# The intra-chunk levels of the gated recurrent heads: products of 64 columns per chunk against products of 128 columns per pair of chunks

## The chip, the cores and the metric

The kernel runs on one core of a Trainium2 chip. The metric is the device time of one execution in microseconds. Three runs of the kernel before took 2513.89, 2510.45 and 2513.90 us; their median is 2513.89 us. A profile of one further execution is read beside them.

The core has four compute engines that run their own queues in order and wait for one another on semaphores: TensorE (PE, matrix products, with a separate weight load, PEld, for each), VectorE (DVE), ScalarE (ACT) and GpSimd (POOL). DMA transfers are issued mostly from SyncE (SP).

## The reference

One transformer-like block over 512 tokens and 2048 features. What bears on this case is the HGRN2 head group: 8 heads of width 128, a gated linear recurrence over the tokens.

```python
qf = silu(q);  log_f = log(lb + (1 - lb) * sigmoid(f_pre));  kf = (1 - lb) * sigmoid(-f_pre)
b = cumsum(log_f within a chunk)
# inside a chunk, for t >= s, per channel k of the head:
att[t, s] = sum_k q[t, k] * kf[s, k] * exp(b[t, k] - b[s, k])
out[t] = sum_s att[t, s] * v[s] + (q[t] * exp(b[t])) @ state
state  = exp(b_last) * state + sum_s (kf[s] * exp(b_last - b[s])) v[s]^T
```

Around it stand a modulated norm, an input projection of 7184 columns, a Mamba-2 head group (SSD), a gate and output projection, and a gated feed-forward network with 5632 hidden features. Everything is float32.

## The kernel before

**Projections.** Every large product is computed in float32 accuracy out of three products of a faster type. `wchunk` (L139) loads two 128-row pieces of a weight into a `raw` buffer, casts them to a high part on ACT (`whi`, L161) and forms the low part on DVE (`wlo`, L162); two buffers each hold them. `mm3` (L165 to L168) then issues three matmuls of 512 columns into a PSUM accumulator: high by high, high by low, low by high. `feat_group` (L621) and `tok_group` (L643) run over the weight's chunks; a chunk is eight calls of `mm3`.

**Small work between the large.** After each `mm3` the kernel calls `small()` (L601). Two generators are active at a time, taken from a list `waiting`; `small()` lets one of them issue its next step, in turn, and a generator that has yielded n sits out n calls. So the products of the recurrent heads (`hgrn_mix`, L526) and of the SSD heads (`ssd_mix`) are strewn singly between projection products. Per chunk, `tick()` (L214) advances the modulation sums (`mod_unit`, L174): each step fetches 512 KB of `w_mod` into a `raw` buffer and adds it up on DVE in `macc` (L187, L189). `rate` sets how many steps a chunk makes: 0.5 while the heads' f and q columns are projected, 1.5 from the z groups on. The order in which the groups run is: the first projection segments, the second v group, four groups for f and q of two heads each, two z groups, two gate groups, the output projection, the feed-forward network. The engines' queues are ordered when the kernel is built: among the instructions that the builder's model holds ready, the one that stands earliest in the program goes first.

**A recurrent head.** `hgrn_f` and `hgrn_q` (L514 to L524) turn the projected columns, which lie as 128 channels by 512 tokens, into the gate `f`, the key `k` and the query `q`. In `hgrn_mix` the tokens form four chunks of 128. The pair products of a chunk are built in levels 1, 2, 4, ..., 64. At level lv, tokens are taken in blocks of 2 lv: the queries of a block's second half meet the keys of its first half. So per level and chunk there is one product (L547) with `k` of the chunk, 128 columns, as weights, and the 64 second-half queries of the chunk as the moving operand. The four results fill 256 columns of one PSUM bank. Then DVE does four things: it multiplies the second-half queries by the gate product of the first half (L552), the first-half keys by that of the second half (L553), copies from PSUM into `att` under a mask that keeps each block's own pairs (L555), and multiplies the two gate products of a block into one (L557), in place, so that the running products stand at every 2 lv-th token (`tcur`). After the seven levels `k` holds what the state needs and `q` what meets the state. Then come the transposes of `k` (L563), the state products with `v` (L570), the state sums on DVE (L573, L575), and the output products, `att` by `v` and `q` by state (L581, L584), copied out by ACT (L589).

**Buffers.** `T()` (L65) takes tiles from a ring of nine of 512 columns, shared by `q`, `att`, `Kt`, `st` and the z and gate groups' `zs`, `gs`. `MIS()` (L77) takes one of two PSUM banks for all small products. `f` and `k` of two heads share an `FK` tile, two of which exist together with the SSD heads' `xdt`. The projections have six PSUM banks.

**Masks.** `level_masks` (L666) builds one int8 mask of 128 x 256 per level on POOL (L672, L674).

Of the kernel before, what the change touches and what calls it, by code (L numbers as in the profile page):

```python
# [34 lines left out]
def hybrid_block_kernel(  # L35
# [55 lines left out]

    ident = CT([P, P], "ident")
    make_identity(nc, ident)
    ones = CT([P, P], "ones")
    V.memset(ones, 1.0)
    tri = CT([P, P], "tri")
# [414 lines left out]
    def ov(t):  # L511
        return otile[t // 2].rearrange("p (t f) -> p t f", t=2)[:, t % 2, :]

    def hgrn_f(ps, h, f, k):  # L514
        A.activation(out=f, in_=ps, func=AF.Sigmoid)
        V.tensor_scalar(out=f, in0=f, scalar1=omlT[:, h:h + 1], scalar2=lbT[:, h:h + 1], op0=ALU.mult, op1=ALU.add)
        A.activation(out=k, in_=ps, func=AF.Sigmoid, scale=-1.0)
        V.tensor_scalar(out=k, in0=k, scalar1=omlT[:, h:h + 1], scalar2=None, op0=ALU.mult)

    def hgrn_q(ps):  # L520
        q = T("q")
        A.activation(out=q, in_=ps, func=AF.Sigmoid)
        V.tensor_tensor(out=q, in0=q, in1=ps, op=ALU.mult)
        return q  # L524

    def hgrn_mix(h, f, k, q):  # L526
# [9 lines left out]
                        in1=ident.unsqueeze(1).broadcast_to([P, 4, P]), op=ALU.mult)  # L536
        V.tensor_tensor(out=q, in0=q, in1=f, op=ALU.mult)
        yield 2
        tcur = f
        for lv in LEVELS:  # L540
            nb = S // (2 * lv)
            ps = MIS()
            npc = P // (2 * lv)
            qv = q.rearrange("p (b two j) -> p b two j", two=2, j=lv)
            kv = k.rearrange("p (b two j) -> p b two j", two=2, j=lv)
            for cch in range(4):
                PE.matmul(out=ps[:, cch * 64:(cch + 1) * 64], lhsT=k[:, cch * P:(cch + 1) * P],  # L547
                          rhs=qv[:, cch * npc:(cch + 1) * npc, 1, :], start=True, stop=True)
                if cch < 3:
                    yield 0  # L550
            tv = tcur.rearrange("p (b two) -> p b two", two=2)
            V.tensor_tensor(out=qv[:, :, 1, :], in0=qv[:, :, 1, :], in1=bc(tv[:, :, 0], [P, nb, lv]), op=ALU.mult)  # L552
            V.tensor_tensor(out=kv[:, :, 0, :], in0=kv[:, :, 0, :], in1=bc(tv[:, :, 1], [P, nb, lv]), op=ALU.mult)  # L553
            av = att.rearrange("p (b two j) -> p b two j", two=2, j=lv)[:, :, 1, :]
            V.copy_predicated(out=av, mask=lmask[lv].rearrange("p (b j) -> p b j", j=lv),  # L555
                              data=ps[:, 0:256].rearrange("p (b j) -> p b j", j=lv))
            V.tensor_tensor(out=tv[:, :, 0], in0=tv[:, :, 0], in1=tv[:, :, 1], op=ALU.mult)  # L557
            tcur = tv[:, :, 0]
            yield 2
        kt_ = T("Kt")[:, 0:3 * P]  # L560
        ps = MIS()
        for cch in range(3):
            PE.transpose(out=ps[:, cch * P:(cch + 1) * P], in_=k[:, cch * P:(cch + 1) * P], identity=ident)  # L563
            yield 0
        A.copy(out=kt_, in_=ps[:, 0:3 * P])
        yield 1
# [6 lines left out]
        V.tensor_copy(out=st[:, 0:P], in_=ps[:, 0:P])  # L573
        for cch in (1, 2):
            V.scalar_tensor_tensor(out=st[:, cch * P:(cch + 1) * P], in0=st[:, (cch - 1) * P:cch * P],  # L575
                                   scalar=tcur[:, cch:cch + 1], in1=ps[:, cch * P:(cch + 1) * P],
                                   op0=ALU.mult, op1=ALU.add)
        po = MIS()
        for cch in range(4):
            sl = slice(cch * P, (cch + 1) * P)  # L580
            PE.matmul(out=po[:, sl], lhsT=att[:, sl], rhs=vt[:, cch, :], start=True, stop=(cch == 0))  # L581
            yield 0
            if cch > 0:
                PE.matmul(out=po[:, sl], lhsT=q[:, sl], rhs=st[:, (cch - 1) * P:cch * P], start=False, stop=True)  # L584
                yield 0
        if not otile:
            otile.extend([E(name="o"), E(name="o")])
# [6 lines left out]
            A.activation(out=junk, in_=ov(cch)[:, h * P:(h + 1) * P], func=AF.Square, accum_out=sq[:, cch:cch + 1])  # L594
        r = rstd_of(sq, 4, P)
        V.tensor_copy(out=orstd[:, h, :], in_=r)


    active, waiting = [], []
# [61 lines left out]
    def bl(i):  # L661
        return slice(i * P, (i + 1) * P)
# [3 lines left out]
    def level_masks():  # L666
        one8 = tmp.tile([P, 256], I8, tag="t", name="one8")
        V.memset(one8, 1)
        for h in LEVELS:
            nb = P // (2 * h)  # L670
            m = CT([P, 256], f"lm{h}", I8)
            G.affine_select(out=m, in_=one8, pattern=[[0, 4], [-2 * h, nb], [0, h]], base=0,  # L672
                            channel_multiplier=1, compare_op=ALU.is_ge, fill=0.0)
            G.affine_select(out=m, in_=m, pattern=[[0, 4], [2 * h, nb], [0, h]], base=h - 1,  # L674
                            channel_multiplier=-1, compare_op=ALU.is_ge, fill=0.0)
            lmask[h] = m


# [94 lines left out]
    for pr in range(4):  # L773
        h0 = 2 * pr
        rate[0] = 0.5
        accs = feat_group([(C_F + P * h0, 256), (C_Q + P * h0, 256)], [bl(i) for i in range(4)])
        fkt = E(name="FK", tag="a").rearrange("p (a s) -> p a s", a=4)
        for i in range(2):
            f_, k_ = fkt[:, 2 * i, :], fkt[:, 2 * i + 1, :]
            hgrn_f(accs[i], h0 + i, f_, k_)  # L780
            waiting.append(hgrn_mix(h0 + i, f_, k_, hgrn_q(accs[2 + i])))
# [256 lines left out]
```

## Time and profile before

| quantity | value |
| --- | --- |
| median of three runs | 2513.89 us |
| profiled execution, its own time | 2516.08 us |
| profiled execution, span | 2514.4 us |
| mean granted clock of TensorE | 0.988 |
| first and last level product (L547) | 469.4 and 794.7 us |
| last copy of a head's output (L589) | 824.4 us |
| level products: instructions, mean duration | 448, 251 ns |

The profile counts an instruction as busy from its start to its (modelled) end; consecutive matmuls overlap, so that starts, not durations, tell what one costs. An f32 product appears as two matmul instructions with a weight load each. A window of the profile lists the busy time of the engines in that stretch, and how many instructions they ran in it. A wait is listed with the engine that ended it.

### The profile page before, as it was taken

To read this page: it belongs to the slowest core of one execution; us is meant where nothing else is said; L and a number is where in the kernel's file an instruction comes from. 1 tells how busy PE (TensorE), PEld (TensorE's weight loads), DVE (VectorE), ACT (ScalarE), POOL (GpSimd) and SP (SyncE) were. 2 spreads that over 40 slices of the span, in tenths; PEclk is the share of its full clock that TensorE was granted. 3 is DMA by queue.
4 is the path that set the end of the run, shared out by engine and by line. 5 is a ranking of instruction groups with operands and counts; after the bars stand their busy time and mean duration, and the time that the engine had idled before them with its cause. 6 is when DMAs were issued, how large, how long until landed. Compare 5 with 4: busy or idle time off the path is not lost.

```text
span 2514.4 us, 29234 instructions
## 1 busy us (share of the span) xinstructions
PE 2443.9 (97%) x11287; PEld 2015.4 (80%) x11287; DVE 1497.7 (60%) x2253; ACT 754.8 (30%) x1035; POOL 54.1 (2%) x66
## 2 busy tenths in 40 slices
PE   6999998999999999999999999999999999999998
PEld 5777877788878777887888888888888888888887
DVE  6884866556767656587636363635454545454557
ACT  6323422221322432332222222222222222232323
POOL 4000000000000000000000000000000000000000
PEclk8999999999999999999999999999999999999999
DMA  8893575335455666466323332333323232323242
GB/s 272 263 280 107 113 125 106 96 109 151 144 159 155 235 198 200 140 203 230 98 95 98 95 101 93 100 94 99 97 96 101 92 101 93 101 93 100 96 130 85
DMA packets 262823, 335.87 MB, mean 134 GB/s; under 512 B 18092, under 2 KB 182524, under 8 KB 261404
## 3 DMA queue, kind: packets, MB, share of 16 engines
q1 hardware_dynamic: 260432, 327.42, 41.5%
q0 software_dynamic: 1568, 4.31, 2.3%
q10 hardware_dynamic: 684, 2.28, 0.3%
q8 instruction: 88, 1.44, 0.2%
q14 instruction: 51, 0.42, 0.0%
HBM read 329.72 MB, written 4.23 MB: 133 GB/s over the span
## 4 chain that ended last, share of the span: by engine, by line
PE 81%; DMA 9%; DVE 7%; ACT 2%; issue 1%; SPq 0%; POOL 0%; ACTq 0%; DVEq 0%; POOLq 0%
PE acc L166 26%; PE acc L168 25%; PE acc L167 25%; DMA m<-in_w_mod_dram 7%; DVE wlo L162 2%; PE mis L547 2%; DVE macc L189 1%; DVE macc L238 1%; DMA raw<-in_w_in_dram 1%; ACT whi L161 1%; DMA x<-in_x_dram 1%; DMA mm<-acrow 0%; PE mis L201 0%; PE mis L487 0%; POOL rstd L265 0%
## 5 line engine op out<-in xcount | busy, mean ns | idle before, releaser
L162 DVE TENSOR_TENSOR wlo<-raw,whi 128x1024 fp32r<-128x1024 f32 (+1 forms) x408 | 490.4, 1203 | 744.9 <-ACT whi L161 739.3
L161 ACT CAST whi<-raw 128x1024 fp32r<-128x1024 f32 (+2 forms) x416 | 424.3, 1021 | 1403.3 <-PE acc L167 596.5
L166 PE MATMUL acc<-hhi,whi 128*128 128x512 f32 x1920 | 770.0, 402 | 11.7 <-ACT whi L161 7.1
L168 PE MATMUL acc<-hhi,wlo 128*128 128x512 f32 x1920 | 751.6, 394 | 3.6 <-DVE wlo L162 3.4
L167 PE MATMUL acc<-hlo,whi 128*128 128x512 f32 x1920 | 753.0, 392 | 0.0
L166 PEld LDWEIGHTS acc<-hhi,whi 128*128 128x128 f32 x1920 | 362.9, 189 | 87.2 <-ACT whi L161 11.2
L168 PEld LDWEIGHTS acc<-hhi,wlo 128*128 128x128 f32 x1920 | 362.4, 189 | 83.1 <-DVE wlo L162 6.5
L167 PEld LDWEIGHTS acc<-hlo,whi 128*128 128x128 f32 x1920 | 363.3, 189 | 67.9 <-issue 0.2
L166 PE MATMUL acc<-whi,act 128*128 128x512 f32 x640 | 249.0, 389 | 0.0
L167 PE MATMUL acc<-wlo,act 128*128 128x512 f32 x640 | 249.0, 389 | 0.0
L168 PE MATMUL acc<-whi,act 128*128 128x512 f32 x640 | 249.0, 389 | 0.0
L189 DVE SCALAR_TENSOR_TENSOR macc<-m,cT,macc 128x512 f32<-128x512 f32 x240 | 179.9, 750 | 106.8 <-DMA m<-in_w_mod_dram 102.6
L166 PE MATMUL acc<-whi,hhi 128*128 128x512 f32 x384 | 168.6, 439 | 0.0
L168 PE MATMUL acc<-whi,hlo 128*128 128x512 f32 x384 | 154.8, 404 | 0.0
L167 PE MATMUL acc<-wlo,hhi 128*128 128x512 f32 x384 | 154.0, 401 | 0.0
L166 PEld LDWEIGHTS acc<-whi,act 128*128 128x128 f32 x640 | 120.1, 188 | 25.0
L168 PEld LDWEIGHTS acc<-whi,act 128*128 128x128 f32 x640 | 120.1, 188 | 25.0
L167 PEld LDWEIGHTS acc<-wlo,act 128*128 128x128 f32 x640 | 120.1, 188 | 24.9
L950 DVE TENSOR_TENSOR g<-acc,gate 128x512 f32<-128x512 f32 x160 | 105.2, 683 | 3.9
L166 PE MATMUL acc<-mhi,whi 128*128 128x512 f32 x256 | 105.2, 411 | 0.0
L547 PEld LDWEIGHTS mis<-q,FK 128*128 128x128 f32 x448 | 83.5, 191 | 27.1 <-issue 8.3
L951 DVE TENSOR_TENSOR x<-x,g 128x512 f32<-128x512 f32 x160 | 105.1, 682 | 0.0
(263 smaller groups left out, 2249.8 us busy)
## 6 DMA issues: line engine op xcount, KB each, us to landing
raw<-in_ffn_w_up_dram SPq DMA_DIRECT2D x352, 256.0 KB, 2.9
m<-in_w_mod_dram SPq DMA_DIRECT2D x128, 512.0 KB, 4.3
raw<-in_ffn_w_down_dram SPq DMA_DIRECT2D x88, 512.0 KB, 3.6
m<-in_w_mod_dram SPq DMA_DIRECT2D x128, 256.0 KB, 4.3
raw<-in_w_in_dram SPq DMA_DIRECT2D x96, 256.0 KB, 3.5
raw<-in_w_in_dram SPq DMA_DIRECT2D x48, 512.0 KB, 3.8
raw<-in_w_out_dram SPq DMA_DIRECT2D x32, 512.0 KB, 4.6
x<-in_x_dram SPq DMA_DIRECT2D x8, 1024.0 KB, 10.6
```

What stands on the lines that cost most here:

```text
L161: A.copy(out=h_, in_=r_)
L162: V.tensor_tensor(out=l_, in0=r_, in1=h_.bitcast(F32), op=ALU.subtract)
L166: PE.matmul(out=ps, lhsT=lh, rhs=rh, start=first, stop=False)
L167: PE.matmul(out=ps, lhsT=lh, rhs=rl, start=False, stop=False)
L168: PE.matmul(out=ps, lhsT=ll, rhs=rh, start=False, stop=last)
L189: V.scalar_tensor_tensor(out=acc, in0=last[:, k, :], scalar=cT[:, kt:kt + 1], in1=acc, op0=ALU.mult, op1=ALU.add)
L238: V.scalar_tensor_tensor(out=acc, in0=m[:, k, :], scalar=cT[:, kt:kt + 1], in1=acc, op0=ALU.mult, op1=ALU.add)
L547: PE.matmul(out=ps[:, cch * 64:(cch + 1) * 64], lhsT=k[:, cch * P:(cch + 1) * P], rhs=qv[:, cch * npc:(cch + 1) * npc, 1, :], start=True, ...
L950: V.tensor_tensor(out=m, in0=accs[t], in1=gates[5][:, cs], op=ALU.mult)
L951: V.tensor_tensor(out=x1[t][:, cs], in0=x1[t][:, cs], in1=m, op=ALU.add)
```

## The change

The four chunks of a head are kept in another order and, the odd ones, backwards in time. Slot 0 and 1 of `f`, `k`, `q` and `att` hold chunks 0 and 2 forwards, slots 2 and 3 hold chunks 1 and 3 with their tokens reversed. In a reversed chunk the first half of a block (in time) lies at the places where an even chunk has its second half. So the first-half keys of an even chunk and those of the odd chunk beside it fit into one weight tile of 128 columns (64 from each), and the 64 + 64 second-half queries are one moving operand of 128 columns: one product for a pair of chunks and a level. Half of each product (even keys by odd queries, and the reverse) isn't wanted, and the masks leave it out.

What this needs besides:

- `kk`, a copy of the first-half keys on ACT, one per level and head, as contiguous weights;
- sigmoids and the `q` product in two instructions each, one for the even and one for the odd chunks, the latter written backwards;
- `flip_v`, once per group of four heads: the two odd token blocks of `v` are reversed by a product with a flipped identity, and copied back by ACT;
- `fwd`: `att` and `q` of the odd chunks are turned forwards by two ACT copies before the output products;
- masks in two halves (28 selects on POOL, not 14);
- the level's DVE instructions in another order: `k`, `q`, the masked copy, the gates. The wait after a level becomes 3 calls of `small()`, and a wait of 1 is added before the output products.

The core of the diff:

```diff
+    flip = CT([P, P], "flip")
+    V.tensor_copy(out=flip, in_=ident[:, ::-1])
...
+    def slot(cch):
+        return slice((cch % 2 * 2 + cch // 2) * P, (cch % 2 * 2 + cch // 2 + 1) * P)
+    def in_slots(dst, src):
+        d = dst.rearrange("p (e c s) -> p e c s", e=2, c=2)
+        i = src.rearrange("p (c e s) -> p c e s", e=2, c=2)
+        return ((d[:, 0, :, :], i[:, :, 0, :]), (d[:, 1, :, ::-1], i[:, :, 1, :]))
+    def halves(t, lv, second, inner=None, base=0, pairs=2):
+        a = t[:, 0:S]
+        es = S // 2 - lv if second else S // 2 + lv
+        inner = [1, lv] if inner is None else inner
+        dims = [list(a.ap[0]), [es, 2], [2 * lv, pairs * P // (2 * lv)]] + [inner]
+        return bass.AP(tensor=a.tensor, offset=a.offset + base + (lv if second else 0), ap=dims)
...
     def hgrn_q(ps):
         q = T("q")
-        A.activation(out=q, in_=ps, func=AF.Sigmoid)
-        V.tensor_tensor(out=q, in0=q, in1=ps, op=ALU.mult)
+        for o, i in in_slots(q, ps):
+            A.activation(out=o, in_=i, func=AF.Sigmoid)
+        for o, i in in_slots(q, ps):
+            V.tensor_tensor(out=o, in0=o, in1=i, op=ALU.mult)
...
         for lv in LEVELS:
...
-            for cch in range(4):
-                PE.matmul(out=ps[:, cch * 64:(cch + 1) * 64], lhsT=k[:, cch * P:(cch + 1) * P],
-                          rhs=qv[:, cch * npc:(cch + 1) * npc, 1, :], start=True, stop=True)
-                if cch < 3:
+            kk = T("kk")[:, 0:256]
+            A.copy(out=kk.rearrange("p (b e j) -> p e b j", e=2, j=lv), in_=halves(k, lv, False))
+            ps = MIS()
+            for pr in range(2):
+                o = ps[:, 0:256].rearrange("p (e c b j) -> p e c b j", e=2, c=2, j=lv)[:, :, pr, :, :]
+                PE.matmul(out=o, lhsT=kk[:, pr * P:(pr + 1) * P], rhs=halves(q, lv, True, base=pr * P, pairs=1),
+                          start=True, stop=True)
+                if pr == 0:
                     yield 0
...
-            yield 2
+            q2, k1 = halves(q, lv, True), halves(k, lv, False)
+            V.tensor_tensor(out=k1, in0=k1, in1=halves(f, lv, True, inner=[0, lv]), op=ALU.mult)
+            V.tensor_tensor(out=q2, in0=q2, in1=halves(f, lv, False, inner=[0, lv]), op=ALU.mult)
+            V.copy_predicated(out=halves(att, lv, True), mask=lmask[lv].rearrange("p (e b j) -> p e b j", e=2, j=lv),
+                              data=ps[:, 0:256].rearrange("p (e b j) -> p e b j", e=2, j=lv))
+            fb = f.rearrange("p (e b two j) -> p e b two j", e=2, two=2, j=lv)
+            V.tensor_tensor(out=fb[:, :, :, 0, 0], in0=fb[:, :, :, 0, 0], in1=fb[:, :, :, 1, 0], op=ALU.mult)
+            yield 3
...
+        fwd = T("fwd")
+        for n, o in enumerate((att, q)):
+            A.copy(out=fwd[:, n * 256:(n + 1) * 256].rearrange("p (c s) -> p c s", c=2),
+                   in_=o[:, 256:512].rearrange("p (c s) -> p c s", c=2)[:, :, ::-1])
...
+        yield 1
...
+    def flip_v(grp):
+        for t in (1, 3):
+            v = vtiles[grp][:, t * 512:(t + 1) * 512]
+            ps = MIS()
+            PE.matmul(out=ps, lhsT=flip, rhs=v, start=True, stop=True)
+            A.copy(out=v, in_=ps)
+            yield 0
...
+            for e in range(2):
+                me = m[:, e * P:(e + 1) * P]
+                G.affine_select(out=me, in_=one8[:, 0:P], pattern=[[0, 2], [-2 * h, nb], [0, h]], base=-e * h,
+                                channel_multiplier=1, compare_op=ALU.is_ge, fill=0.0)
+                G.affine_select(out=me, in_=me, pattern=[[0, 2], [2 * h, nb], [0, h]], base=h - 1 + e * h,
+                                channel_multiplier=-1, compare_op=ALU.is_ge, fill=0.0)
...
         accs = feat_group([(C_F + P * h0, 256), (C_Q + P * h0, 256)], [bl(i) for i in range(4)])
+        if pr % 2 == 0:
+            waiting.append(flip_v(pr // 2))
```

`hgrn_f` splits its two sigmoids in the same way as `hgrn_q`.

## What the change was expected to do

> **What bounds the kernel now.** I read the page first: busy shares, then the chain of work that ended last.
>
> ```profile
> span 2514.4 us, 29234 instructions
> ...
> PE 2443.9 (97%) x11287; PEld 2015.4 (80%) x11287; DVE 1497.7 (60%) x2253; ACT 754.8 (30%) x1035; POOL 54.1 (2%) x66
> ...
> PE 81%; DMA 9%; DVE 7%; ACT 2%; issue 1%; SPq 0%; POOL 0%; ACTq 0%; DVEq 0%; POOLq 0%
> ```
>
> TensorE is busy 97% of the span and carries 81% of the chain. The page warns that a busy PE need not be PE at its peak, so the question is whether the products that the change removes take time on PE that nothing else could use. Next comes the table of groups, kept apart by shape, for the level products (L547):
>
> ```profile
> L547 PEld LDWEIGHTS mis<-q,FK 128*128 128x128 f32 x448 | 83.5, 191 | 27.1 <-issue 8.3 <-PE acc L168 0.5 <-DVE att L555 0.4
> L547 PE MATMUL mis<-q,FK 128*128 128x64 f32 x448 | 75.6, 251 | 3.6 <-DVE q L537 3.4
> ```
>
> There are 448 instructions for 8 heads x 7 levels x 4 chunks = 224 products: an f32 product is two passes, each with its own weight load. Then the busy time by stretches, over the part in which the recurrent heads run, and around it:
>
> ```profile
> 462.00:826.00 364.00, 359.48 (x1917) 301.10 (x1916) 244.22 (x499) 94.37 (x203) 11.93 (x9) 0.99 0.47 141
> ```
> ```profile
> 668.00:704.00 36.00, 36.00 (x196) 30.36 (x195) 29.61 (x70) 8.38 (x18) 1.64 (x1) 1.00 0.54 168
> ```
> ```profile
> 720.00:740.00 20.00, 16.08 (x83) 12.93 (x81) 12.87 (x27) 10.90 (x42) 5.22 (x3) 0.98 0.44 136
> 740.00:760.00 20.00, 20.00 (x95) 16.38 (x94) 12.95 (x26) 2.09 (x2) 0.00 (x0) 0.85 0.46 132
> ```
>
> The columns are the stretch, its length, PE, PEld, DVE, ACT, POOL busy, granted clock, DMA share and GB/s. In the 364 us of the heads PE idles 4.5 us in all, and 3.9 of these lie in 720-740. DVE stands at 67%, ACT at 26%. So this stretch is bound by PE, and a product less on PE is time less, at the price of one product's slot.
>
> **What one slot costs.** The order in time on PE (start, duration, engine, line) shows it; durations overlap, so I go by starts.
>
> ```profile
> 556.34 0.40 PE L166 MATMUL acc<-hhi,whi 128*128 128x512 f32 x1
> ...
> 557.03 0.40 PE L166 MATMUL acc<-hhi,whi 128*128 128x512 f32 x1
> ...
> 557.50 0.40 PE L168 MATMUL acc<-hhi,wlo 128*128 128x512 f32 x1
> 557.73 0.33 PE L547 MATMUL mis<-q,FK 128*128 128x64 f32 x2
> ...
> 558.41 0.40 PE L168 MATMUL acc<-hhi,wlo 128*128 128x512 f32 x1
> ```
> ```profile
> 541.60 0.40 PE L168 MATMUL acc<-hhi,wlo 128*128 128x512 f32 x1
> 541.84 0.38 PE L584 MATMUL mis<-st,q 128*128 128x128 f32 x2
> ...
> 542.52 0.39 PE L168 MATMUL acc<-hhi,wlo 128*128 128x512 f32 x1
> ```
>
> Three matmuls of the projection (one call of `mm3`) take 557.03 - 556.34 = 0.69 us alone; over a stretch without small products it is 0.68:
>
> ```profile
> 1300.00:1400.00 100.00, 100.00 (x443) 82.81 (x442) 49.36 (x62) 24.84 (x27) 0.00 (x0) 1.00 0.31 99
> ```
>
> that is 443 matmuls in 100 us, 0.226 each. With a 64-column product between them the period is 558.41 - 557.50 = 0.91, with a 128-column product 542.52 - 541.60 = 0.92. So both widths cost the same slot, **0.24 us**: the width is free at this size, the number of products is what PE pays for. That is the heart of the change.
>
> **The change part by part.**
>
> *Products removed.* 224 become 112; each of the 112 that stay is 128 columns wide and keeps its 0.24. Saved: 112 x 0.24 = **26.9 us**.
>
> *Flipping v.* `flip_v` adds four f32 products of 512 columns. The nearest is L196, in the chain (start, us, what):
>
> ```profile
> 1170.85 0.86 PE mis L196 x2
> ```
>
> 0.86 a product: 4 x 0.86 = **+3.4 us** of PE. Its four ACT copies are on an idle engine.
>
> *DVE.* Level work keeps its four instructions and their 256 columns (the last shrinks by level as before), with other strides. Groups of DVE in 462-826:
>
> ```profile
> L189 DVE SCALAR_TENSOR_TENSOR macc<-m,cT,macc 128x512 f32<-128x512 f32 x91 | 68.2, 750 | 20.7 <-DMA m<-in_w_mod_dram 18.9
> L162 DVE TENSOR_TENSOR wlo<-raw,whi 128x1024 fp32r<-128x1024 f32 x48 | 58.7, 1224 | 55.6 <-ACT whi L161 54.9 <-DMA raw<-in_w_in_dram 0.7
> L555 DVE COPY_PREDICATED att<-lm,mis 128x256 f32<-128x256 int8 x56 | 28.9, 516 | 0.0
> L552 DVE TENSOR_TENSOR q<-q,FK 128x256 f32<-128x256 f32 x56 | 23.6, 421 | 17.2 <-PE mis L547 17.0
> L553 DVE TENSOR_TENSOR FK<-FK 128x256 f32<-128x256 f32 x56 | 23.4, 417 | 0.0
> L557 DVE TENSOR_TENSOR FK<-FK 128x256 f32<-128x256 f32 (+6 forms) x56 | 15.2, 271 | 0.0
> ...
> L523 DVE TENSOR_TENSOR q<-q,acc 128x512 f32<-128x512 f32 x6 | 4.1, 683 | 0.4 <-ACT q L522 0.4
> ```
>
> One level of one head is 516 + 421 + 417 + 271 = 1.63 us busy. The only new DVE time is `hgrn_q`: 8 of 683 become 16 of about 421, +1.3 us, hidden today. What changes is density. `small()` issues one step per `mm3`, alternating between two heads. Counting yields, a level takes both heads 8 calls today, and 5 after the change (two products each, then a wait of 3). A level of both heads had 8 x 0.68 + 8 x 0.24 = 7.4 us on PE; it will have 5 x 0.68 + 4 x 0.24 = 4.4. Seven levels: 30.6 us of PE, in which DVE must do 14 x 1.63 = 22.8 of level work, 35/8 x 1.22 = 5.3 of `wlo`, and the modulation sums at 0.75: at `rate` 0.5 (first two pairs of heads) 35/8 x 1 x 0.75 = 3.3, at 1.5 (the last two pairs) 9.8. Sum 31.4 or 37.9, against 30.6. Starts of neighbouring DVE instructions lie closer than their durations, which the next rows show: 0.34 apart at 0.42 long, 1.57 a level at the first level.
>
> ```profile
> 563.62 0.42 DVE L552 TENSOR_TENSOR q<-q,FK 128x256 f32<-128x256 f32 x1 [0.85 <-PE mis L547]
> 563.96 0.42 DVE L553 TENSOR_TENSOR FK<-FK 128x256 f32<-128x256 f32 x1
> ...
> 565.19 0.41 DVE L552 TENSOR_TENSOR q<-q,FK 128x256 f32<-128x256 f32 x1
> ```
>
> Taking 0.08 off each level instruction gives 26.9 and 33.4. So DVE becomes **as tight as PE** here: its lateness over four pairs is between 0 + 2 x 2.8 = 6 and 2 x 0.8 + 2 x 7.3 = 16 us. PE pays only the part for which a level product at its place in PE's queue waits: behind it are projection matmuls that need none of it. Today such waits sum to 8.3 us at L547's weight loads and 3.4 at its matmuls (rows above). Against it, `k`'s product now stands ahead of `q`'s and needs no result of PE, and the wait is 3 calls, not 2. Bounds: 0 to +16; I take **+4**, near the low end, since modulation sums can slide.
>
> *ACT.* New: 56 copies `kk`, 16 `fwd`, 4 flips, and 24 sigmoids of 512 split into 48 of 256.
>
> ```profile
> L793 ACT ACTIVATE zs<-y 128x256 f32<-128x256 f32 x16 | 6.5, 409 | 1.8 <-DVE y L791 1.8
> ...
> L589 ACT COPY o<-mis 128x256 f32<-128x256 f32 x16 | 5.2, 377 | 5.6 <-PE mis L584 5.6
> ...
> L515 ACT ACTIVATE FK<-acc 128x512 f32<-128x512 f32 x8 | 4.8, 599 | 18.7 <-PE acc L168 7.6 <-PE mis L487 7.0 <-DVE st L575 4.2
> ...
> L718 ACT COPY v<-acc 128x512 f32<-128x512 f32 x8 | 4.4, 593 | 3.4 <-PE acc L168 2.3 <-PE mis L497 0.8
> ```
>
> 72 x 0.38 + 4 x 0.59 + 48 x 0.41 - 24 x 0.60 = 35 us, so ACT goes from 94 to 129 of some 340: covered. The copy is a new wait: ACT stands at it until DVE has written `k` of the level before, and behind it stand `whi` casts, for which DVE's `wlo` and then the projection wait; with two `whi` buffers that cast runs a chunk (5.4 us or more) ahead, which covers it. The other way round, a `kk` copy can stand behind a cast that waits for PE, and the product that wants it waits too. Without any cover 56 x 0.38 = 21 us would come onto PE. I put it inside the +4, because the copy's input is written first of the level's four. Reversed writes are not in this trace; I price them as straight ones, and at double they add under 20 us to a one-third-filled ACT, nothing to PE.
>
> *Less cover later.* By the same count the heads end at call 475, not 546, of the 576 from the second v group to the end of the gate groups (today's last copy of a head is at 824.4 us). About 70 calls of the gate groups lose their small products while each chunk still fetches 1.5 modulation pieces. The out projection already runs so:
>
> ```profile
> 890.00:990.00 100.00, 97.74 (x456) 78.58 (x455) 58.12 (x75) 28.91 (x37) 0.00 (x0) 1.00 0.60 194
> ```
>
> PE loses 2.3% there, with the chain in `m<-in_w_mod`; 70 x 0.68 = 48 us at 2 to 4%: **+1.5 us** (0 to 3).
>
> *Masks and `flip`.* 14 POOL selects become 28 of half the width; the small DMAs behind them go out last on POOL, and ACT is the first to want one:
>
> ```profile
> L672 POOL TENSOR_SCALAR_AFFINE_SELECT lm<-one 128x256 int8<-128x256 int8 x7 | 9.3, 1340 | 4.7 <-DVE one L668 4.7
> ...
> L674 POOL TENSOR_SCALAR_AFFINE_SELECT lm<-lm 128x256 int8<-128x256 int8 x7 | 8.2, 1191 | 0.1
> ```
> ```profile
> 51.98 0.57 POOL L739 DMA_DIRECT2D ph<-in_ssd_dt_bias_dram  x1
> ```
> ```profile
> L743 ACT ACTIVATE an<-ph x1: 219/219/219, 75.2 to 75.2; 128x16 f32<-128x16 f32 x1
> ```
>
> If each half still took the whole time, the DMAs would go 17.5 us later, at 69.5, with 5.7 left. No cost taken, 0 to +3. The one DVE copy that makes `flip` falls into a hole that DVE has anyway (11.3 us before this row):
>
> ```profile
> 14.78 0.69 DVE L284 COPY xT<-acc 128x512 f32<-128x512 f32 x1 [11.30 <-PE acc L278]
> ```
>
> *The tile ring.* At a head's end `q`, `att`, `st` and now `fwd` live: two heads 8, two waiting `q` 2, of 9 buffers. By the count this happens as the first z group ends and wants buffers for its `zs`. Today the two ends meet at the second z group, which is the hole at 720-740: 3.9 us idle, and then a clock of 0.85 for 20 us, 3 more. One such hole is traded for another: 0, with -7 to +7 as bounds. [...]
>
> **Sum.** -26.9 + 3.4 + 4 + 1.5 = **-18 us**. The profiled execution took 2516.08 (span 2514.4), 2.2 above the median of the three runs, 2513.89. So 2498 for it, **2496** for the median. About 5 us (0.2%) is what a measurement of this kernel can tell from none.
>
> **Rivals.**
>
> 1. *DVE takes over.* All 16 us of lateness reach PE, since in the dense levels each product waits for `q`: -26.9 + 3.4 + 16 + 1.5 = -6, 2508. For it: 37.9 against 30.6. Against it: in 668-704, among levels, DVE runs at 82% and PE at 100%. Chance 0.15.
>
> 2. *All of it arrives.* Nothing late, the hole gone without a successor: -26.9 + 3.4 - 7 = -30.5, 2483. Chance 0.12.
>
> 3. *The wide product streams slowly* (slower). Each level product reads `q` with gaps and now writes PSUM in two runs. From L196 a pass runs at 0.43 us per 512 columns, 0.107 per 128; two fit the slot. At half pace, 64 columns take 0.107 and would fit today's slot unseen, but 128 take 0.215, the slot 0.24 + 0.215 = 0.455: 112 x 0.215 = +24, a sum of +6, 2520. It turns from gain to loss where the slot passes 0.24 + 18/112 = 0.40. No row has a 128-column product with gapped operands, so the trace can't exclude it. But the write breaks only once in 128 columns, and the reads of levels 2 to 64 come in runs: level 1 alone, 16 products, would cost 3.4. Chance 0.08. [...]
>
> 4. *The removed slots were cover* and PE finds another limit (the modulation stream) at once: -18 shrinks to within 5 us. Against it: 0.47 DMA share, 141 GB/s, in the row of 462-826. Chance 0.05.
>
> My forecast, 2488 to 2505: 0.60. The range for 8 in 10 reaches to most of rival 1 and half of rival 2: **2485 to 2512**. Faster by over 0.2%: 0.80; within: 0.11; slower: 0.09.
>
> **What would show it.** Right: 224 level instructions of 128 columns on PE instead of 448, the slot still 0.24 between starts; heads ending near 750 us; DVE near 80% or more in the levels, PE still near full; waits of PE for `q` or `kk` at a few us. Wrong: a slot above 0.3; PE waits at the level products above 15 us; idle on `kk`; PE idle from `m` in the gate groups above 5 us; new holes with a lower clock behind them.

## The result and the profile after

| | before | after |
| --- | --- | --- |
| median of four runs | 2513.89 us (2510.45 to 2516.95) | 2495.36 us (2491.69 to 2497.32) |
| profiled execution, its own time | 2516.08 us | 2497.32 us |
| profiled execution, span | 2514.4 us | 2495.6 us |
| mean granted clock of TensorE | 0.988 | 0.991 |

The ratio after to before is 0.9925, with a 95% interval of 0.9907 to 0.9943: 18.5 us less by the medians, 18.8 by the spans. The forecast was 2496 us.

The page of the kernel after: span, busy time of the engines (share of the span, instructions) and the shares of the chain that ended last.

```profile
span 2495.6 us, 28998 instructions
...
PE 2416.4 (97%) x11071; PEld 1987.7 (80%) x11071; DVE 1490.2 (60%) x2262; ACT 783.7 (31%) x1135; POOL 55.7 (2%) x80
...
PE 76%; DMA 11%; DVE 9%; issue 2%; ACT 2%; POOL 0%; SPq 0%; DVEq 0%; ACTq 0%; POOLq 0%
```

TensorE has 11287 - 11071 = 216 instructions less: 224 less at the level products and 8 more for the four flips of `v`. It is still busy for 97% of a shorter span, but its share of the chain fell from 81 to 76%; DMA and DVE gained two points each. Something beside the products has come onto the path.

The groups of the kernel after, by shape (busy us and mean ns of one, then the idle time ahead of them and what ended it). The level product is L570 now; L577, L576, L566 and L575 are the masked copy, the `q` product, the `kk` copy and the `k` product, L634 the flip.

```profile
L570 PE MATMUL mis<-q,kk 128*128 128x128 f32 x224 | 43.9, 278 | 3.2 <-DVE att L577 1.8 <-DVE q L562 0.8 <-DVE FK L580 0.3
L570 PEld LDWEIGHTS mis<-q,kk 128*128 128x128 f32 x224 | 40.6, 188 | 16.5 <-issue 6.8 <-ACT whi L163 1.2 <-ACT kk L566 0.3
L577 DVE COPY_PREDICATED att<-lm,mis 128x256 f32<-128x256 int8 x56 | 29.1, 520 | 0.0
L576 DVE TENSOR_TENSOR q<-q,FK 128x256 f32<-128x256 f32 x56 | 23.6, 422 | 5.8 <-PE mis L570 5.7
L566 ACT COPY kk<-FK 128x256 f32<-128x256 f32 x56 | 22.1, 416 | 55.9 <-DVE FK L575 47.0 <-PE mis L570 7.8 <-DVE wlo L164 1.0
L575 DVE TENSOR_TENSOR FK<-FK 128x256 f32<-128x256 f32 x56 | 21.8, 422 | 0.3
...
L634 PE MATMUL mis<-v,flip 128*128 128x512 f32 x8 | 4.1, 592 | 0.0
```

224 instructions of 128 columns stand where 448 of 64 stood. One lasts 278 ns and not 251, but durations overlap; the order in time on TensorE of the kernel after (start, duration) tells what it costs:

```profile
560.81 0.39 PE L170 MATMUL acc<-hhi,wlo 128*128 128x512 f32 x1
561.04 0.38 PE L570 MATMUL mis<-q,kk 128*128 128x128 f32 x2
...
561.72 0.40 PE L170 MATMUL acc<-hhi,wlo 128*128 128x512 f32 x1
...
598.08 0.39 PE L170 MATMUL acc<-hhi,wlo 128*128 128x512 f32 x1
598.31 1.02 PE L634 MATMUL mis<-v,flip 128*128 128x512 f32 x2
...
599.64 0.40 PE L170 MATMUL acc<-hhi,wlo 128*128 128x512 f32 x1
```

From one L170 to the next, with a level product between, are 0.91 us, as before with half the columns. Over all periods of three projection matmuls and one level product the median of the starts is 0.920 before (212 periods) and 0.920 after (105). A flip costs 599.64 - 598.08 - 0.69 = 0.87.

Then the time by stretches (length, PE, PEld, DVE, ACT and POOL busy with instructions, granted clock, DMA share, GB/s). The first stretch runs from the first f and q group to the end of the gate groups, the second is the output projection. Before:

```profile
354.50:845.70 491.20, 476.27 (x2472) 396.74 (x2472) 321.90 (x645) 129.24 (x248) 18.91 (x18) 0.98 0.50 136
...
845.70:1058.40 212.70, 205.54 (x996) 166.39 (x994) 124.62 (x171) 68.95 (x96) 1.01 (x1) 0.99 0.59 195
```

After, with the two z groups by themselves between:

```profile
353.30:825.30 472.00, 450.30 (x2256) 370.72 (x2255) 316.89 (x650) 158.38 (x348) 18.18 (x18) 0.99 0.50 141
...
600.80:722.60 121.80, 117.38 (x605) 96.54 (x603) 98.72 (x219) 43.97 (x109) 5.08 (x4) 0.99 0.53 160
...
825.30:1039.80 214.50, 205.06 (x995) 166.46 (x993) 125.30 (x173) 68.96 (x96) 1.01 (x1) 0.99 0.59 195
```

In the first stretch TensorE is busy 476.27 - 450.30 = 26.0 us less, and idle 14.9 us before, 21.7 after: **26.0 less busy, 6.8 more idle, 19.2 less**. The output projection gives back 1.8. Ahead of the stretch 1.2 go, in the feed-forward network 0.2: 19.2 + 1.2 - 1.8 + 0.2 = 18.8, the difference of the spans.

Where TensorE waits is in the list of its waits (what waits, who ended it: us, times, longest), from the third f and q group to the end of the gate groups. Before (L547 is the level product):

```profile
PE mis L547 <- DVE q L537: 3.4, 2, 3.0
PE mis L532 <- ACT o L589: 0.9, 1, 0.9
```

After (L612 output product, L859 transposes for the output projection, L203 end of a modulation sum):

```profile
PE mis L612 <- DVE st L597: 3.9, 2, 2.0
PE mis L859 <- DVE mlo L861: 2.4, 1, 2.4
PE mis L570 <- DVE att L577: 1.8, 3, 0.9
PE mis L203 <- DVE st L597: 1.4, 1, 1.4
PE mis L570 <- DVE q L562: 0.8, 1, 0.8
PE mis L570 <- DVE FK L580: 0.3, 1, 0.3
```

4.3 us became 10.6. The three large waits that are new end with the state sums (L597) or with `mlo`: not in the levels, but at a head's end and in the output projection's preparation. One of them from both sides, first TensorE, then DVE, in order of time (the bracket gives idle time before, and what ended it):

```profile
655.51 0.39 PE L169 MATMUL acc<-wlo,hhi 128*128 128x512 f32 x1
657.32 1.05 PE L203 MATMUL mis<-ones,macc 128*128 128x1 f32 x8 [1.42 <-DVE st L597]
```
```profile
656.25 0.75 DVE L191 SCALAR_TENSOR_TENSOR macc<-m,cT,macc 128x512 f32<-128x512 f32 x1 [1.72 <-DMA m<-in_w_mod_dram]
656.92 0.34 DVE L597 SCALAR_TENSOR_TENSOR st<-st,FK,mis 128x128 f32<-128x128 f32 x1
```

A modulation sum (L191) waits for its transfer, 1.72 us. The state sum, which reads one of the two PSUM banks of the small products, stands behind it in DVE's queue and starts at 656.92. TensorE's next small product wants that bank and waits until 657.32, and the projection products behind it wait too. The hole that ends at 581.97 (1.88 us) has the same form: there DVE waits 2.16 us for a piece `m`, then runs a `wlo`, then the state sum. At 735.29 (2.04) and 780.40 (2.43) DVE is busy, with norm products and a `wlo`, ahead of the state sum or `mlo`. It came late to this work: it had waited 1.75 us for POOL's `rstd`, until 731.00, and 2.65 us for a piece `m`, until 774.38.

DVE's own waits for `m` between 450 and 1040 us grew: from 71.0 + 14.8 = 85.8 us before to 98.0 + 17.5 = 115.5 after.

### The profile page after: what moved, and what is told of

It is laid out like the page before. It is cut to its first block, busy times and chain, and to the rows that moved or that the text cites. A ratio compares the mean times of both kernels' runs of the same rounds, so it can differ in the third digit from the quotient of the medians.

```text
span 2495.6 us, 28998 instructions
## 1 busy us (share of the span) xinstructions
PE 2416.4 (97%) x11071; PEld 1987.7 (80%) x11071; DVE 1490.2 (60%) x2262; ACT 783.7 (31%) x1135; POOL 55.7 (2%) x80
## 4 chain that ended last, share of the span: by engine, by line
PE 76%; DMA 11%; DVE 9%; issue 2%; ACT 2%; POOL 0%; SPq 0%; DVEq 0%; ACTq 0%; POOLq 0%
PE acc L170 24%; PE acc L168 24%; PE acc L169 24%; DMA m<-in_w_mod_dram 8%; DVE wlo L164 3%; DVE macc L191 2%; DMA raw<-in_w_in_dram 1%; DVE macc L240 1%; DMA x<-in_x_dram 1%; ACT whi L163 1%; PE mis L570 1%; POOL rstd L267 0%; DMA mm<-acrow 0%; PE mis L612 0%; DVE att L577 0%
## 5 line engine op out<-in xcount | busy, mean ns | idle before, releaser
L170 PE MATMUL acc<-hhi,wlo 128*128 128x512 f32 x1920 | 750.1, 393 | 3.1 <-DVE wlo L164 3.1
L168 PEld LDWEIGHTS acc<-hhi,whi 128*128 128x128 f32 x1920 | 362.2, 189 | 88.2 <-ACT whi L163 10.2
L170 PEld LDWEIGHTS acc<-hhi,wlo 128*128 128x128 f32 x1920 | 362.3, 189 | 83.0 <-DVE wlo L164 6.1
L191 DVE SCALAR_TENSOR_TENSOR macc<-m,cT,macc 128x512 f32<-128x512 f32 x240 | 180.0, 750 | 127.9 <-DMA m<-in_w_mod_dram 124.5
L170 PE MATMUL acc<-whi,act 128*128 128x512 f32 x640 | 249.0, 389 | 0.0
L168 PE MATMUL acc<-whi,hhi 128*128 128x512 f32 x384 | 163.2, 425 | 0.0
L170 PE MATMUL acc<-whi,hlo 128*128 128x512 f32 x384 | 153.7, 401 | 0.0
L170 PEld LDWEIGHTS acc<-whi,act 128*128 128x128 f32 x640 | 120.1, 188 | 25.0
L170 PE MATMUL acc<-mhi,wlo 128*128 128x512 f32 x256 | 101.1, 395 | 2.3 <-DVE wlo L164 2.3
```

Of the source, the lines that this page charges most:

```text
L168: PE.matmul(out=ps, lhsT=lh, rhs=rh, start=first, stop=False)
L170: PE.matmul(out=ps, lhsT=ll, rhs=rh, start=False, stop=last)
L191: V.scalar_tensor_tensor(out=acc, in0=last[:, k, :], scalar=cT[:, kt:kt + 1], in1=acc, op0=ALU.mult, op1=ALU.add)
```

## The experiments

Times are medians in us, ratios against the kernel before, run on the same chip (its medians there were 2513.37 to 2514.06).

| run | based on | median (lowest to highest) | ratio, 95% interval |
| --- | --- | --- | --- |
| e1_double | after | 2517.16 (2512.24 to 2521.35) | 1.0011 (0.9999 to 1.0022) |
| e2_wide | before | 2519.74 (2516.54 to 2524.42) | 1.0019 (1.0010 to 1.0029) |
| e3_kk_twice | after | 2495.11 (2489.26 to 2498.49) | 0.9917 (0.9897 to 0.9936) |
| e4_wait5 | after | 2493.04 (2485.95 to 2494.06) | 0.9901 (0.9880 to 0.9922) |
| e5_rate | after | 2497.10 (2495.49 to 2500.51) | 0.9933 (0.9921 to 0.9945) |
| e6_both | after | 2498.88 (2489.57 to 2501.37) | 0.9933 (0.9920 to 0.9947) |
| e8_kept_after | after | 2480.86 (2477.10 to 2482.17) | 0.9863 (0.9848 to 0.9877) |
| e9_kept_before | before | 2510.20 (2507.72 to 2513.15) | 0.9984 (0.9975 to 0.9993) |
| e10_rate_late | after | 2497.21 (2491.87 to 2501.89) | 0.9931 (0.9916 to 0.9946) |
| e11_before_late | before | 2514.70 (2510.76 to 2519.48) | 1.0000 (0.9991 to 1.0009) |
| e12_late_wait5 | after | 2499.29 (2492.83 to 2502.92) | 0.9938 (0.9924 to 0.9952) |
| e13_lag | after | 2498.53 (2497.50 to 2500.90) | 0.9943 (0.9929 to 0.9956) |

### Each level product twice

```diff
+                for _ in range(2):
                     PE.matmul(out=o, lhsT=kk[:, pr * P:(pr + 1) * P], rhs=halves(q, lv, True, base=pr * P, pairs=1),
                               start=True, stop=True)
```

> The changed kernel with each of the 112 level products issued twice, one behind the other, at the same step; the second overwrites the first with the same values, so that PE again runs as many level products as before (224), while the order of waits, the copies and the DVE work stay those of the change. Theory A (the gain is PE slots, 0.24 us for each product that is gone): 112 x 0.24 = 26.9 us come back, 2495.4 + 27 = 2522, at or just above the kernel before (ratio to it about 1.003). Theory B (the gain comes from the new order of waits and the earlier end of the heads, and PE had room): within 5 us of the changed kernel, 2490 to 2500, ratio 0.991 to 0.995.

This gives TensorE as many products as before the change, and leaves DVE's and ACT's work alone. Order in time on TensorE, and the first stretch, of this kernel (level product L571):

```profile
575.11 0.39 PE L170 MATMUL acc<-hhi,wlo 128*128 128x512 f32 x1
575.35 0.60 PE L571 MATMUL mis<-q,kk 128*128 128x128 f32 x4
...
576.25 0.39 PE L170 MATMUL acc<-hhi,wlo 128*128 128x512 f32 x1
```
```profile
350.90:846.40 495.50, 477.40 (x2481) 397.67 (x2480) 318.97 (x649) 159.04 (x348) 18.54 (x18) 0.98 0.48 134
```

The period is 1.14 where it was 0.92: a second product right behind the first, with the same weights, costs 0.22. 112 x 0.22 = 24.6. The stretch is 495.5 - 472.0 = 23.5 us longer and the median 21.8. The whole gain is gone, so **the number of products is what the time hangs on**, and they were not cover for something else. The price is a little below the 0.24 of a product that stands alone.

### 128 columns, as many products

```diff
-                PE.matmul(out=ps[:, cch * 64:(cch + 1) * 64], lhsT=k[:, cch * P:(cch + 1) * P],
-                          rhs=qv[:, cch * npc:(cch + 1) * npc, 1, :], start=True, stop=True)
+                PE.matmul(out=ps[:, cch * P:(cch + 1) * P], lhsT=k[:, cch * P:(cch + 1) * P],
+                          rhs=q[:, cch * P:(cch + 1) * P], start=True, stop=True)
```

The masked copy reads every second block of the bank.

> The kernel before with each of its 224 level products widened from 64 to 128 columns: the moving operand is the whole chunk of queries, the result fills a whole PSUM bank, and the masked copy takes every second block from it. Theory A (a slot of 0.24 us is set by the two weight loads, and the width is free up to 128): 2514 within 5 us, ratio 0.998 to 1.002, and the period of three projection matmuls with one product stays 0.92 us. Theory C (columns cost their stream time): two passes of 64 more columns at 0.43/512 us a column are 0.107 us a product, 224 x 0.107 = 24 us, 2538, period 1.03 us.

Order in time on TensorE of this kernel, and the waits of the level products' weight loads:

```profile
560.83 0.40 PE L168 MATMUL acc<-hhi,wlo 128*128 128x512 f32 x1
561.07 0.38 PE L547 MATMUL mis<-q,FK 128*128 128x128 f32 x2
...
561.75 0.39 PE L168 MATMUL acc<-hhi,wlo 128*128 128x512 f32 x1
```
```profile
PEld mis L547 <- issue: 18.7, 32, 3.4
```

0.92 again, over 217 periods: twice the columns at the same slot. A price on width, which would have put the period at 1.03, is out. Yet the run is longer than the kernel before, by 6.4 us in the medians and 4.2 in the profiled spans; the two z groups are 5.2 longer (62.5 and 61.5 us, against 60.2 and 58.6). Weight loads of the level products wait 18.7 us where the kernel before has 8.3. Why these rose **stays open**; the number of products is that of the kernel before, so it does not touch the slot.

### The `kk` copy twice

```diff
+            for _ in range(2):
                 A.copy(out=kk.rearrange("p (b e j) -> p e b j", e=2, j=lv), in_=halves(k, lv, False))
```

> The changed kernel with each of the 56 copies of the first-half keys made twice into the same tile, so that ACT has 56 x 0.42 = 23 us more and the product that waits for the copy can start 0.3 to 0.4 us later. Theory A (the copy is covered: ACT idles two thirds of this stretch and the copy's input is written first): 2495 to 2499, ratio 0.992 to 0.995, waits of PE for kk below 2 us. Theory D (the copy lies in the chain from level to level and was part of the 4 us of lateness): 28 levels of two heads at 0.3 to 0.4 us are 8 to 11 us if the two heads' copies overlap, 17 to 22 if not: 2504 to 2517.

The group of this kernel, and what its level products' weight loads wait for:

```profile
L567 ACT COPY kk<-FK 128x256 f32<-128x256 f32 x112 | 42.4, 419 | 42.5 <-DVE FK L576 37.4 <-PE mis L571 2.8 <-DVE wlo L164 0.6
```
```profile
PEld mis L571 <- ACT kk L567: 1.3, 4, 0.5
```

20.3 us more on ACT, each copy on the way to a level product, cost nothing in the median (2495.11 against 2495.36). Weight loads wait 1.3 us in all for `kk` (0.3 with one copy). The copy is covered.

### A longer wait after a level, and an even rate

`yield 3` after a level becomes `yield 5`; in the other run the modulation sums run at one rate throughout, not 0.5 and then 1.5; the third has both.

```diff
-            yield 3
+            yield 5
```
```diff
-        rate[0] = 0.5
+        rate[0] = 1.125
...
-    rate[0] = 1.5
+    rate[0] = 1.125
```

> The changed kernel with a wait of 5 calls after each level, not 3: by the count of calls a level of two heads takes 7 calls, not 5, the heads end at call 508 of 576, not 475, so that DVE's level work is thinner (7 x 0.68 + 4 x 0.24 = 5.7 us of PE a level against 4.4) and more of the gate groups keep their small products. Theory A (DVE's density makes the level products wait, and the cover of the gate groups is lost): waits at the level products fall from 10 us (3.2 at matmuls, 6.8 at weight loads) to below 4, and 3 to 6 us are gained: 2489 to 2492. Theory E (PE idles because DVE stands in order at modulation sums that wait for their DMA, whatever the level density): the holes move but stay, 2493 to 2498.

> The changed kernel with the modulation pieces spread evenly, 1.125 a chunk from the f and q groups to the end of the output projection, in place of 0.5 and then 1.5: the same 108 steps. Theory E: PE idles less in the z and gate groups and the output projection (16 us there now), 4 to 8 us gained, 2487 to 2491; in the f and q groups DMA is at 0.4 of its time and has room. Theory A: the dense levels in the f and q groups get 2.25 sums a chunk in place of 1, DVE needs 31 us of 30.6 there, and what is gained later is lost there: 2493 to 2498.

> The changed kernel with both: the wait of 5 calls after a level and the even rate of 1.125. If the wait of 5 removed holes of the one kind (6 us less idle in the stretch of the heads) and the rate those of the other, the two add: 2482 to 2488, ratio to the kernel before 0.988 to 0.990. If both remove the same holes: 2488 to 2493.

With the longer wait the first stretch falls to 465.5 us, of which 15.5 idle (21.7 without):

```profile
355.50:821.00 465.50, 450.02 (x2258) 372.53 (x2256) 318.57 (x651) 158.19 (x348) 18.49 (x18) 0.99 0.51 142
```

But the waits at the level products, which the longer wait was to cure, are about as before (weight loads 3.9 + 3.2 us, matmuls 2.3 + 0.7 + 0.3 + 0.3; without it 6.8 + 0.3 and 3.2). What is gone are the holes at the state sums. The other stretches give back 3 us, and the intervals of the two ratios overlap: this is not told apart from the kernel after.

The even rate moves time instead of saving it. The first two f and q groups, in which the SSD heads run, take 68.5 + 74.6 us and not 59.8 + 71.4, and the granted clock in most of that stretch is 0.94, where the kernel after has 0.97 from 353.3 to 487.1:

```profile
351.20:485.00 133.80, 118.75 (x558) 96.37 (x558) 87.45 (x165) 34.81 (x53) 5.96 (x8) 0.94 0.59 136
```

The output projection, with fewer sums in it, takes 209.0 us and not 214.5. Modulation sums cost where they are put. Both edits together (2498.88) give neither the sum of the two nor the better one.

### Without the modulation's transfers, in both kernels

```diff
+    kept = []
...
-            if q < 8:
-                m = wst.tile([P, 2, 512], F32, tag="raw", name=nm("m"))
+            if q < 8 and not kept:
+                m = wst.tile([P, 2, 512], F32, tag="kept", name=nm("m"), bufs=1)
...
+                kept.append(m)
+            m = kept[0]
```

The modulation parts 2 to 5 are summed from one piece of `w_mod`, fetched once, and all their other transfers are left out; DVE does the same sums. One `raw` buffer is taken away (four, not five) for the kept one. The same edit goes into the kernel before. Ahead of the first stretch both get some 10 us longer (it starts at 365.0 and 364.5 us, not at 353.3 and 354.5), so their medians do not show all that the edit gains in the stretch.

> The changed kernel with the modulation sums (parts 2 to 5) taken from one piece of w_mod that is loaded once and kept, so that DVE's sums have the same instructions and never wait for a transfer; this leaves out the other pieces, and one of the five raw buffers holds the kept piece. Theory E (the idle time that PE gained after the change comes from DVE standing in order at sums whose piece hasn't landed, with state sums and masked copies behind them): from the f and q groups of heads 4 and 5 to the output projection PE's idle time falls from 20 us (2.1, 2.0, 2.4, 2.0, 2.4 and 9.5 by stage) to below 8, and that stretch is 10 us shorter or more. Theory A (DVE's density): the holes in the z groups stay, idle there above 4 us. The stages ahead of the second v group may be longer, with a raw buffer less.

> The same edit in the kernel before. If the 0.24 us a product is all that the change is worth where nothing else gets in the way, the stretch from the first f and q group to the output projection is 23 to 26 us longer here than in the changed kernel with the same edit (26.9 for 112 products, less 3.5 for the flips); with the transfers it was 19.2. The hole of 3.9 us at the start of the gate groups should shrink if it came from the transfers, and stay if it came from the tile ring and the norm at that place.

The first stretch and the output projection, first of the changed kernel without the transfers, then of the kernel before without them:

```profile
365.00:822.60 457.60, 448.04 (x2256) 371.44 (x2255) 307.62 (x634) 158.18 (x348) 18.57 (x18) 0.99 0.31 80
822.60:1026.50 203.90, 201.84 (x996) 165.35 (x994) 136.89 (x188) 69.57 (x96) 1.01 (x1) 1.00 0.31 106
```
```profile
364.50:848.70 484.20, 472.74 (x2474) 394.98 (x2472) 309.56 (x627) 129.17 (x248) 18.07 (x18) 0.99 0.29 76
848.70:1052.60 203.90, 201.87 (x995) 165.23 (x992) 136.75 (x188) 69.46 (x96) 1.01 (x1) 1.00 0.31 106
```

TensorE's waits in the same part as above, in the same order:

```profile
PE mis L616 <- DVE st L601: 1.2, 1, 1.2
PE mis L574 <- DVE q L566: 1.1, 1, 1.1
PE mis L574 <- DVE att L581: 0.5, 2, 0.3
```
```profile
PE mis L551 <- DVE q L541: 2.9, 2, 1.8
PE mis L551 <- DVE FK L561: 0.2, 1, 0.2
```

Without transfers the change is worth 484.2 - 457.6 = **26.6 us** in the stretch, with them 19.2. It no longer adds waits (3.1 us before, 2.8 after; with transfers 4.3 and 10.6). The change's ratio is then 0.9863 / 0.9984 = 0.988; the worst ends of the two intervals give 0.9855 to 0.9902, outside the 0.9907 to 0.9943 of the change with them. So **the transfers of the modulation take some 7 us of the change's gain** by the stretches of one execution each; by the medians it is 11 (2510.20 - 2480.86 = 29.3, against 18.5). The output projection is the same in both, 203.9 us, and pays 8.8 us (before) and 10.6 us (after) for the transfers.

### Moving or decoupling the modulation sums

The other runs were to win these 7 us back. Late rate: 0.5 for the first two f and q groups, then 1.25 to the end; alone, in the kernel before, and with the wait of 5.

```diff
-        rate[0] = 0.5
+        rate[0] = 0.5 if pr < 2 else 1.25
...
-    rate[0] = 1.5
+    rate[0] = 1.25
```

> The changed kernel with the modulation pieces at 0.5 a chunk in the first two f and q groups (where the even rate of 1.125 made the SSD heads wait, 12 us longer) and at 1.25 from the third to the end of the output projection: the same 108 steps. Theory E: the stretch from the third f and q group to the feed-forward network gets 8 to 12 us shorter, as with the even rate, and the first two groups stay as they are: 2484 to 2489, ratio to the kernel before 0.988 to 0.990. If only the sum of late pieces counts and they are late in the third and fourth group instead: 2493 to 2498.

> The kernel before with the same late rate. Its PE idles little in the z and gate groups (4.3 us, of which 3.9 in one hole) and 7.2 us in the output projection, so less is to be had: 2506 to 2513. If theory E holds, the change is then worth 22 to 26 us between this kernel and the changed one at the same rate, in place of 18 to 19.

> The changed kernel with the late rate and a wait of 5 calls after each level. With the pieces spread, the wait of 5 should have few holes left to remove: within 3 us of the same kernel with a wait of 3. If the levels' density counts by itself, 3 to 6 us faster than that.

None gains. The kernel before is at 1.0000 with it, the kernel after at 0.9931, beside 0.9925 without; between the two the change is worth 2514.70 - 2497.21 = 17.5 us, where 22 to 26 had been expected. Moving the sums did not make DVE wait less for their pieces: from 350 to 1040 us it waits 128.3 + 24.5 us in e10_rate_late, 110.5 + 17.5 in the kernel after. So the run does not tell what those waits cost. In the kernel after the first z group gets shorter (56.4 us, from 60.0), and others get longer by as much: the stretch takes 471.2 us, the output projection 215.3. With the wait of 5 on top it is 0.9938; what that wait seemed to give alone does not come back.

Lag: each piece is added up two steps after its transfer is issued, not one.

```diff
-        last = None
-        for q in range(9):
+        held = []
+        for q in range(10):
...
-            for k in range(2 if q else 0):
-                kt = 2 * q - 2 + k
+            for k in range(2 if q > 1 else 0):
+                last = held[q - 2]
+                kt = 2 * q - 4 + k
...
-            last = m
+            held.append(m)
```

> The changed kernel with each modulation piece added up two steps after its transfer is issued, not one, so that DVE should find it landed; a piece then holds its raw buffer a step longer, out of five that it shares with the weights. If it is DVE's standing in order at a sum that costs the time (theory E, first form): DVE's wait for the pieces falls from 124 us to under 60, PE's idle time from the third f and q group to the output projection from 18 us to under 10, 2483 to 2490. If it is the transfers that are late as such, with the buffers full (second form): the waits move to the weights' casts or low parts, 2494 to 2505.

DVE's wait for `m` did not shrink: 99.8 + 17.1 us, against 98.0 + 17.5, and the stretch takes 471.5 us. The edit therefore did not decouple the sums from the transfers, and it can't tell whether DVE's standing in line or the transfers' lateness itself is at fault. That **stays open**. The waits of SyncE's queue, which issues the fetches (L184), show a likely reason: the fetch itself waits for DVE to free a `raw` buffer. In the kernel after, from 490 to 1040 us:

```profile
SPq L184 <- DVE wlo L164: 79.0, 32, 6.1
SPq L184 <- DVE macc L191: 67.8, 42, 6.5
```

With the lag they are 77.3 and 67.9. If a piece is fetched late because DVE is late, a sum that comes a step later need not find it landed; this is read from the waits, and no run tested it. No version that fetches all its pieces is shown to be faster than the changed kernel.

## Why the prediction was right

| step | predicted, us | measured, us |
| --- | --- | --- |
| 112 products less | -26.9 | 112 x 0.22 = -24.6 from the doubled product, up to -26.9 |
| four flips | +3.4 | 4 x 0.87 = +3.5 |
| DVE late at the level products | +4 (0 to 16) | waits there did not grow |
| less cover in the gate groups | +1.5 | idle there 3.9 before (the hole of the next row), 4.5 after (two holes, at 735 and 780) |
| the hole at 720-740, another in its place | 0 (-7 to +7) | four holes of 1.4 to 2.4, 7.8 together, instead of 3.9 us; 3.4 us at half clock behind them, not 6.8 |
| half clock ahead of the levels, not in the sum | 0 | 6.8 us less of it, at most -3.4 |
| output projection, not in the sum | 0 | +1.8 |
| sum | -18 | -18.5 (medians), -18.8 (spans) |

**Slot and width: right.** The period of three projection products and a level product is 0.920 at 64 and at 128 columns, in the changed kernel as in the one with the same number of wide products. So rival 3 is out: a write in two runs of 64 columns shows no loss (0.91 to 0.92 a period), and neither does the gapped read of `q`: the period is 0.92 in e2_wide, which reads `q` without gaps, and 0.93 after at level 1, which reads every second column (from the L170 at 470.36 us to the one at 471.29). That the two weight loads set the slot, as theory A of e2_wide has it, no run shows: a product has two of them in every kernel here.

**The removed products were time: right.** Putting them back (each twice) takes the whole gain away, and in the pair without transfers TensorE's busy time differs by 472.74 - 448.04 = 24.7 us, where products less flips were put at 23.5. Rival 4 in its full form falls; but a part of it is true: some 7 us are lost to the modulation's transfers. That they are lost through DVE's queue is read from the trace of the holes, not shown by a run.

**ACT, masks, flips: right.** 35 us more on ACT had been forecast, 158.38 - 129.24 = 29 came, and doubling the copy changed nothing. The small DMA behind the masks went out at 53.3 us instead of 51.98, and nothing waited for it. The last copy of a head's output ends at 749.5 (near 750 forecast).

**DVE as tight as TensorE: the density was right, the place wrong.** DVE is busy 98.72 of 121.8 us in the z groups, 81%. But the step that made +4 of it, lateness *at the level products*, failed: the idle time ahead of their matmuls is 3.2 us (3.6 before), ahead of their weight loads 16.5 (27.1). Rival 1's 16 us are nowhere. The waits arose at the state sums and at `mlo` instead, where a PSUM bank is held until DVE comes to them; two of the four holes have a modulation sum that waits for its transfer directly in front, a third a little earlier, and without the transfers the change adds no waits. The prediction had noted that modulation sums can slide, as a help. It had not asked who stands behind one that waits.

**The tile ring: not seen.** The hole at 720-740 has gone and others came, as the step said, but their releasers are the state sums and `mlo`, not a buffer of the ring. In the kernel before without the transfers TensorE still waits 2.9 us there, of 3.9, so the transfers made only a small part of the old hole.

So the sum is right partly because errors cancel: TensorE's idle time grew by 6.8 us in the stretch and 2.3 in the output projection (7.16 to 9.44), against +5.5 forecast for all. On the other side the time at a granted clock of 0.5 in the stretch fell from 20.4 to 10.2 us. It is 3.4 us at 381, 6.8 at 432, 3.4 at 449 and 6.8 at 739 before, and 3.4 each at 431, 448 and 659 after. In the piece at 659 the projection matmuls start 0.43 us apart (659.91, 660.33, 660.76), and 0.23 apart at full clock. If TensorE had work all the time, the 10.2 us less would be worth half, an estimated 5.1.

Of these 10.2 us, 6.8 lie ahead of the first level product (469.4 us before, 468.8 after), so they have nothing to do with the products that are gone. The piece at 381 comes and goes: e2_wide and e11_before_late, built on the kernel before, have none there, and e4_wait5, built on the kernel after, has one at 382. No experiment tested what sets these pieces, and the prediction had no term for those ahead of the levels. To that extent the close sum is luck. Between the two kernels without transfers the difference is 3.4 us (13.6 and 10.2), so the clock does not explain why that pair lies further apart.

## What to carry to other kernels

Where small products are strewn between large ones, take their price from the starts of the large ones; here an f32 product cost 0.24 us at 64 and at 128 columns, so halving the number pays and halving the width does not. When such products go, look at which other engine's queue the same work is now packed into, and in it for instructions that wait for a transfer: what stands behind them may hold a buffer that the bound engine wants. Leaving one stream out of both kernels tells how much of a change's gain that stream takes.

## What the hardware showed beside

- A second f32 product with the same weights right behind the first costs 0.22 us, hardly less than one between other products (0.24).
- Copies on ACT that gather or reverse take up to a tenth longer: 416 ns for `kk` and 405 for `fwd`, against 382 for the straight copy of the same shape, all 128 x 256 in f32. The straight one reads PSUM and the others SBUF, so the pattern's own part isn't told apart.

The groups of ACT in the kernel after:

```profile
L620 ACT COPY o<-mis 128x256 f32<-128x256 f32 x16 | 5.3, 382 | 5.2 <-PE mis L615 5.2
...
L602 ACT COPY fwd<-att 128x256 f32<-128x256 f32 x8 | 3.2, 405 | 11.1 <-PE mis L612 8.7 <-PE mis L592 2.4
```

- The length of a hole alone did not tell what the clock does. Behind the one of 1.42 us at 657.32 the granted clock fell to half for 3.4 us; behind those of 1.88, 2.04 and 2.43 us it did not. These are the 3.4 us in the kernel after, and the 20 us around the end of the hole at 735.29 (the clock is the third number from the end):

```profile
659.40:662.80 3.40, 3.40 (x14) 2.82 (x12) 1.81 (x4) 1.04 (x1) 0.00 (x0) 0.51 0.75 220
735.00:755.00 20.00, 19.71 (x104) 16.70 (x105) 11.47 (x21) 6.68 (x23) 2.43 (x2) 1.00 0.62 185
```

What sets the hole at 657 apart in the trace is that behind it come eight instructions of one column (L203) before the next of 512; whether that is the cause was not tested.
